# Attention's max pass as one stream of chunks, the output projection at a lower rate, background work held back while VectorE's modelled queue is long

## The chip, the core and the metric

The program runs on one core of one Trainium2 chip. The metric is the device time of one execution in microseconds, from the first to the last instruction of the core, launch included. Engines are called by the profile's names: PE (TensorE's matmuls; PEld are its weight loads), DVE (VectorE), ACT (ScalarE), POOL (GpSimd), SP (the queue that issues the DMAs). Each engine works off its own queue in order; between engines there are semaphores.

## What is computed

Two layers over 2048 latent tokens and 256 context tokens. A layer reads its stream through one input projection, and three groups of columns are mixed apart: a gated MLP over chunks (A), attention (B) and a linear recurrence in both directions (C). Their outputs, gated, go through `W_o`, and a layer norm closes the layer. The attention is this:

```python
def one_block(qblk):
    s = jnp.einsum('bqgrd,bkgd->bgrqk', qblk, k).astype(jnp.float32) * scale
    p = jax.nn.softmax(s, axis=-1).astype(v.dtype)
    return jnp.einsum('bgrqk,bkgd->bqgrd', p, v)
...
y = jnp.concatenate([mix_a * jax.nn.silu(a_g), attn * jax.nn.silu(b_g),
                     lru * jax.nn.silu(r_g)], -1) @ w_o
x_new = layer_norm(ALPHA * x + gate[:, None] * y, ln_g, ln_b)
```

There are 8 heads of 64 and 2 key heads; latent queries see 2304 keys, context queries 256. The context stream is only needed by the second layer, so the first layer has nine blocks of 256 queries and the second eight.

## The kernel before

A layer is a z phase (projection, gates, recurrence forward; `z_phase`) and an attention phase (`att_phase`), and only the second is touched. Values are kept as pairs of a high and a low half-precision part, which is why most products come as two or three matmuls.

**Units and steps.** A unit is one head of one block. A latent unit has nine steps, one for every two tiles of 128 keys; a context unit has one. So layer 0 has 584 steps and layer 1 has 576. A step `s` of the main loop writes, in this order:

- `scores` (L1023, L1024): four matmuls of 256 columns into a PSUM tile `stp`, then the exponential on ACT into `P`, which has six buffers (L1027);
- `low` (L1034): `Pl`, what `P` loses when its upper half is read as bfloat16. It runs on POOL or on DVE; `less_busy` chooses by the planner's clocks;
- `attend` of the step four earlier: eight matmuls into `pv` (L1051, L1053);
- pieces of other work, each a Python generator that is advanced so many times per step.

**The max pass.** The softmax needs each query's largest score before its exponential. `maxp(u)` is the generator of unit `u`: for each half of the 256 queries it multiplies against all keys in five chunks (four of 512 columns, one of 256) into PSUM tiles `sps`, of which there are three, and DVE reduces each chunk to `pm` (L940, L942) and the five to one column of `MZ` (L948). After the ten chunks come five empty advances, then two small matmuls `mp` and a copy (L954, L955) that put the negated maxima into row 64 of the query tile, where the score matmuls pick them up. `pace` advances the generators so that a unit's fifteen advances are done two steps before the unit begins; it looks four units ahead, and up to two advances fall into one step. `sps` also serves `mp` and the transposes `ytp`: PE waits when all three tiles are still to be read.

**The other work.** `wo` is the output projection of a block: per half block two tiles of 24 matmuls (L1144 to L1146), three per advance, then three DVE instructions per tile (L1149 to L1154); `affine` (L1161 to L1174) is the layer norm behind it. `wo_prep` makes the two halves of `W_o` (`OH` on ACT, `OL` on DVE, L884, 16 of these), and `wo` isn't advanced before `wo_prep` is done. `lru_back` is the backward recurrence: a scan and a cast on DVE (`hb` L859, `yc` L837) and two POOL instructions (L849, L850) per item. `ahead` (layer 0 alone) prepares the next layer: a first block's input, weights `wh_cc`/`wl_cc`, and `setup` with its small tables (`lwf` by DMA, then `lwh`, `lwl`; L235 to L244). `Rate` turns a number into advances per step: 0.8 for `wo`, 0.5 for `affine`, 0.13 for `lru_back`, 0.35 for `wo_prep`, 0.8 for `ahead`. Two switches empty a generator at once: `wo_prep` at step 136, `lru_back` at step 260.

**The planner's clocks.** `use(engine, cost)` adds an estimated time in us to `vt[engine]`; an engine never lies behind `vt[PE]`. In the kernel before only `less_busy` reads these clocks. They exist while the program is built; on the chip the order is fixed: within the attention phase the four engines get their instructions in the order in which they were written.

## Time and profile before

| | us |
|---|---|
| median of 3 runs | 2898.5 (2898.18 to 2899.23) |
| the profiled execution | 2900.0 |
| its span (first to last instruction) | 2897.9 |
| layer 0, first to last step (584) | 662.9 to 1498.4 |
| layer 1, first to last step (576) | 2076.0 to 2862.0 |
| PE busy | 2699.2 (93%) |
| DVE busy | 1995.7 (69%) |
| POOL busy | 1778.6 (61%) |
| ACT busy | 1342.6 (46%) |

Steps are found in the trace by their score matmuls: the first of every four `stp` matmuls marks a step's start. A stretch of the trace is then named by its steps; "steps 0 to 144" of layer 0 are 662.9 to 861.9 us, of layer 1 2076.0 to 2278.0 us. Matmuls overlap their neighbours, so a matmul's listed duration is longer than the time it takes from the engine; that time is read from one start to the next.

### The profile page before, as it was taken

The page shows a single profiled execution, that of the slowest core. Times are in us where ns is not written, and L with a number is a line of the kernel's source. Part 1 is how long each engine was busy: PE and PEld are TensorE (multiplying, and loading weights), DVE is VectorE, ACT ScalarE, POOL GpSimd, SP SyncE. Part 2 cuts the span into 40 slices and gives each one's busy share as a digit, 9 for nine tenths or more (in the row PEclk, how much of TensorE's full clock was granted, in tenths as well). Part 3 has the DMA queues.
Part 4 walks back from the last instruction along what each step waited for, and adds up shares of the span by engine and source line. Part 5 has one row for each costly group of instructions (what it writes and reads, how often), then busy time and mean ns, then how long its engine had stood idle before and what let it go on. Part 6 is the DMA issues. An engine that isn't in the chain of part 4 may idle for free. (4 is left out here: it accounts for less than half of the span.)

```text
span 2897.9 us, 60732 instructions
## 1 busy us (share of the span) xinstructions
PE 2699.2 (93%) x24121; PEld 1818.4 (63%) x24121; DVE 1995.7 (69%) x4000; ACT 1342.6 (46%) x2513; POOL 1778.6 (61%) x1825
## 2 busy tenths in 40 slices
PE   7999999898899999999998989998879999999998
PEld 3555555556677776777664655554567777777775
DVE  5565554558987777777877565555798876777775
ACT  3444433455544554445433454444555444544452
POOL 3244433347888786677764344334588877887774
PEclk9999999999999999999999999999999999999999
DMA  8232222115331110111114111110433110111001
GB/s 291 89 101 87 94 87 86 50 63 175 118 86 37 45 56 30 60 63 41 49 63 138 46 61 54 64 61 31 146 104 104 58 52 20 49 49 49 23 24 45
DMA packets 113717, 213.61 MB, mean 74 GB/s; under 512 B 13396, under 2 KB 45016, under 8 KB 113432
## 3 DMA queue, kind: packets, MB, share of 16 engines
q1 hardware_dynamic: 111060, 208.84, 21.7%
q8 instruction: 189, 3.10, 0.5%
q10 hardware_dynamic: 2372, 0.89, 0.1%
q14 instruction: 96, 0.79, 0.1%
HBM read 147.54 MB, written 62.14 MB: 72 GB/s over the span
## 5 line engine op out<-in xcount | busy, mean ns | idle before, releaser
L1034 POOL TENSOR_TENSOR Pl<-P 128x512 f16<-128x512 f32 x1131 | 1221.5, 1097 | 336.2 <-ACT P L1027 328.1
L1027 ACT ACTIVATE P<-stp 128x512 f32<-128x512 f32 x1160 | 692.5, 597 | 786.2 <-PE stp L1024 718.4
L942 DVE TENSOR_REDUCE pm<-sps 128x1 f32<-128x256 f32 (+1 forms) x1276 | 751.4, 627 | 272.3 <-PE sps L940 269.5
L1024 PE MATMUL stp<-aQB,KB 65*128 65x256 f16 x2320 | 582.7, 276 | 1.4 <-ACT aQB L955 1.4
L1023 PE MATMUL stp<-aQS,KK 128*128 128x256 f16 x2320 | 580.5, 275 | 0.0
L1051 PE MATMUL pv<-VX,P 128*128 128x129 f16 x4640 | 561.2, 220 | 0.0
L1053 PE MATMUL pv<-VX,Pl 128*128 128x65 f16 x4640 | 529.2, 193 | 6.6 <-DVE Pl L1034 3.5
L940 PE MATMUL sps<-KK,aQS 128*128 128x256 f16 (+1 forms) x1276 | 460.0, 362 | 58.9 <-DVE pm L942 56.2
L1053 PEld LDWEIGHTS <-Pl 128*128 128x128 f16 x4640 | 416.8, 98 | 100.4 <-DVE Pl L1034 4.8
L1051 PEld LDWEIGHTS <-P 128*128 128x128 bf16 x4640 | 431.4, 98 | 63.0 <-issue 48.4
L1024 PEld LDWEIGHTS <-KB 65*128 65x128 f16 x2320 | 228.9, 99 | 92.8 <-issue 2.5
L1023 PEld LDWEIGHTS <-KK 128*128 128x128 f16 x2320 | 230.9, 100 | 83.9 <-issue 14.0
L484 POOL TENSOR_SCALAR xh<-xm 128x512 f16<-128x512 f32 x68 | 45.0, 662 | 290.6 <-ACT xm L481 290.0
L495 PEld LDWEIGHTS <-xh 128*128 128x128 f16 x1040 | 102.4, 98 | 124.5 <-issue 19.0
L497 PEld LDWEIGHTS <-xl 128*128 128x128 f16 x1040 | 102.3, 98 | 122.7 <-issue 2.9
L496 PEld LDWEIGHTS <-xh 128*128 128x128 f16 x1040 | 102.3, 98 | 115.4 <-issue 9.2
L646 PE MATMUL cps<-xh,wh_cc 128*128 128x256 f16 x528 | 149.0, 282 | 3.3 <-POOL xh L484 3.0
L648 PE MATMUL cps<-xh,wl_cc 128*128 128x256 f16 x528 | 148.5, 281 | 3.3 <-DVE wl_cc L158 3.3
L647 PE MATMUL cps<-xl,wh_cc 128*128 128x256 f16 x528 | 148.8, 282 | 0.5 <-DVE xl L485 0.5
L397 POOL TENSOR_SCALAR gt<-gt,sp 128x256 f32<-128x256 f32 x72 | 43.9, 618 | 144.1 <-ACT gt L394 138.2
L940 PEld LDWEIGHTS <-aQS 128*128 128x128 f16 x1276 | 125.6, 99 | 10.3 <-DVE yB L1074 0.2
L719 ACT ACTIVATE uv<-uv 128x512 f32<-128x512 f32 x34 | 21.4, 630 | 207.7 <-DVE uv L718 207.7
(273 smaller groups left out, 5383.1 us busy)
## 6 DMA issues: line engine op xcount, KB each, us to landing
wf<-in_w_in_dram SPq DMA_DIRECT2D x64, 256.0 KB
wga<-in_w_ada_dram SPq DMA_DIRECT2D x32, 512.0 KB
lr<-LRd SPq DMA_DIRECT2D x32, 512.0 KB
SBd<-sbg SPq DMA_DIRECT2D x34, 256.0 KB
QSd<-QS SPq DMA_DIRECT2D x17, 512.0 KB
LRd<-gt SPq DMA_DIRECT2D x34, 256.0 KB
aQS<-QSd SPq DMA_DIRECT2D x17, 512.0 KB
asb<-SBd SPq DMA_DIRECT2D x17, 512.0 KB
```

The source lines that it names most:

```text
L495: T.matmul(ps[:, :w], xh[:, k, ts], wh[:, k, c0:], start=(k == 0), stop=False)
L646: T.matmul(ps, wh[:, k, cs], xh[:, k], start=(k == 0), stop=False)
L647: T.matmul(ps, wh[:, k, cs], xl[:, k], start=False, stop=False)
L648: T.matmul(ps, wl[:, k, cs], xh[:, k], start=False, stop=(k == KC - 1))
L940: T.matmul(ps[:, :w], QS[:, h, t * 128:(t + 1) * 128], KK[:, kv].rearrange("p a b -> p (a b)")[:, k0:k0 + w], start=True, stop=True)
L942: V.tensor_reduce(pm[:, i:i + 1], ps[:, :w], axis=AX, op=OP.max)
L1023: T.matmul(ps[:, i], KK[:, kv, kt], QS[:, h], start=True, stop=False)
L1024: T.matmul(ps[:, i], KB[:, kv, kt], QB[:, h], start=False, stop=True)
L1027: S.activation(P, ps, AF.Exp)
L1034: less_busy(0.6, 1.04, 2.0).tensor_tensor(Pl, P, Ph, op=OP.subtract)
L1051: T.matmul(pv[:, t, 0:129], Ph[:, i, ts], VX[:, kt, kv, 0:129], start=first, stop=False, skip_group_check=True)
L1053: T.matmul(pv[:, t, 64:129], Pl[:, i, ts], VX[:, kt, kv, 64:129], start=False, stop=end, skip_group_check=True)
```

## The change

The max pass is no longer one generator per unit. `stream` yields the chunks of all units one after the other, with no empty advances, and appends the unit to `rows`; `row_out`, called once per step behind the scores, counts three steps down and then writes the unit's `mp` matmuls and the copy (`max_row`). `pace` aims at five steps before the unit's beginning instead of two, looks three units ahead instead of four, and carries at most three advances over.

`Rate` now advances at most once per call and takes an argument `room`: where it is false nothing is advanced, and what is due is kept, up to three. `room(dv, po)` compares the planner's clocks: DVE's less than `dv` us ahead of PE's and POOL's less than `po`. The rates go to 0.64 for `wo` (0.8 before), 0.45 for `wo_prep`, 0.14 for `lru_back`; the order of the last three is changed, and the switch for `lru_back` stands at step 330.

The costs of `use` are new for most DVE work: a chunk of 512 0.60 us (0.59), `OL` 1.1 (0.6), scan and copy 1.2 (0.4), `yc` 0.65 (0.33), an affine instruction 1.05 (0.9), `wl_cc` 1.0 (0.6), a POOL pair of the recurrence 1.8 (1.4). `less_busy` gets (0.8, 1.06, 0.8) for (0.6, 1.04, 2.0): `Pl` goes to DVE when POOL is behind by 0.54 us more than DVE, not 1.56.

No instruction's shape changes, and PE, ACT and SP get the same number of each; DVE gets 42 of the 1160 `Pl`, 29 before.

```diff
-                for t in range(2 if u else 0):
+                for t in range(2):
                     pm = p.tile([128, 5], F32, name="pm", tag="pm", bufs=4)
...
-                        if i < 5 or t == 0:
-                            yield
-                    V.tensor_reduce(mz[:, t, 64:65], pm[:, :i], axis=AX, op=OP.max, negate=True)
-                    use(DV, 0.08)
-                for _ in range(5 if u else 0):
-                    yield
+                        if k0 + 512 >= nk:
+                            V.tensor_reduce(mz[:, t, 64:65], pm[:, :i], axis=AX, op=OP.max, negate=True)
+                            use(DV, 0.1)
+                        yield
...
-                less_busy(0.6, 1.04, 2.0).tensor_tensor(Pl, P, Ph, op=OP.subtract)
+                less_busy(0.8, 1.06, 0.8).tensor_tensor(Pl, P, Ph, op=OP.subtract)
...
+            def stream():
+                for u in range(1, len(units)):
+                    for _ in max_chunks(u):
+                        yield
+                    rows.append([u, 3])
...
+            def row_out(now):
+                for r in list(rows):
+                    r[1] -= 1
+                    if r[1] <= 0 or r[0] <= now:
+                        max_row(r[0])
+                        rows.remove(r)
+                        made[0] = r[0]
...
-                def __call__(self, gens):
-                    self.due += self.rate
-                    n = int(self.due)
-                    self.due -= n
-                    pump(gens, n)
+                def __call__(self, gens, room=True):
+                    self.due = min(self.due + self.rate, 3.0) if gens else 0.0
+                    if self.due >= 1.0 and room:
+                        self.due -= 1.0
+                        pump(gens, 1)
+
+            def room(dv, po=9.0):
+                return vt[DV] - vt[PE] < dv and vt[PO] - vt[PE] < po
...
-                total += 14 if b else 7
-                need[u] = total + 1
-            pumped, due = need[0], 0.0
+                total += (10 if b else 2) if u else 0
+                need[u] = total
+            pumped, due = 0, 0.0
...
-                for u in range(u0 + 1, min(u0 + 5, len(units))):
-                    rate = max(rate, (need[u] - pumped) / max(begin[u] - 2 - s, 1))
-                due += rate
+                for u in range(u0 + 1, min(u0 + 4, len(units))):
+                    rate = max(rate, (need[u] - pumped) / max(begin[u] - 5 - s, 1))
+                due = min(due + rate, 3.0)
...
                     if not preps:
-                        rwo(wos)
+                        rwo(wos, room(2.5))
                         if len(wos) > 1:
                             rwo(wos)
-                    rln(lnq)
-                    if len(lnq) > 1:
-                        rln(lnq)
-                    rback(backs)
-                    rprep(preps)
+                    rln(lnq, room(1.6) or len(lnq) > 1)
+                    rprep(preps, room(1.0))
+                    rback(backs, room(1.0, 2.0))
```

**DVE's queue in layer 0, around step 57.** `pm` are the chunk reductions, `OL` the weights' low half, `hb`, `hbk` and `yc` the recurrence, `rc`, `pv` and `yB` the end of a head. Before:

```order
L884 SCALAR_TENSOR_TENSOR OL<-wof,OH 128x512
L942 TENSOR_REDUCE pm<-sps 128x1 x2
L948 TENSOR_REDUCE MZ_77<-pm 128x1
L1070 RECIPROCAL rc<-pv 128x2
L1071 TENSOR_TENSOR pv<-ol,pv 128x2x64
L1074 SCALAR_TENSOR_TENSOR yB<-pv,rc,asb 128x64 x2
L884 SCALAR_TENSOR_TENSOR OL<-wof,OH 128x512
L837 SCALAR_TENSOR_TENSOR yc<-hb,yc 128x256
L859 SCALAR_TENSOR_TENSOR hb<-lr,hbk 128x256
L863 COPY hbk<-hb 128x1
L942 TENSOR_REDUCE pm<-sps 128x1
```

and now, around step 45, at the first scan of the recurrence in the same layer:

```order
L942 TENSOR_REDUCE pm<-sps 128x1 x3
L947 TENSOR_REDUCE MZ_75<-pm 128x1
L942 TENSOR_REDUCE pm<-sps 128x1 x2
L859 SCALAR_TENSOR_TENSOR hb<-lr,hbc 128x256
L863 COPY hbk<-hb 128x1
L942 TENSOR_REDUCE pm<-sps 128x1
L1036 TENSOR_TENSOR Pl<-P 128x512
L942 TENSOR_REDUCE pm<-sps 128x1 x2
L947 TENSOR_REDUCE MZ_75<-pm 128x1
```

Nine other instructions stood between two reductions; now the pieces of `wo_prep` and `lru_back` stand apart, with reductions between.

**POOL's queue at the start of layer 0's attention**, `Pl` and the pairs of the recurrence. Before:

```order
L1034 TENSOR_TENSOR Pl<-P 128x512 x23
L849 TENSOR_TENSOR hb<-lr 128x256
L850 TENSOR_TENSOR hb<-hb,lr 128x256
L1034 TENSOR_TENSOR Pl<-P 128x512 x6
L849 TENSOR_TENSOR hb<-lr 128x256
L850 TENSOR_TENSOR hb<-hb,lr 128x256
L1034 TENSOR_TENSOR Pl<-P 128x512 x6
```

and now:

```order
L1036 TENSOR_TENSOR Pl<-P 128x512 x21
L849 TENSOR_TENSOR hb<-lr 128x256
L850 TENSOR_TENSOR hb<-hb,lr 128x256
L1036 TENSOR_TENSOR Pl<-P 128x512 x21
L849 TENSOR_TENSOR hb<-lr 128x256
L850 TENSOR_TENSOR hb<-hb,lr 128x256
L1036 TENSOR_TENSOR Pl<-P 128x512 x26
```

The recurrence's pairs have moved from every sixth or seventh `Pl` to every twentieth or so, that is, to later steps.

**DVE's queue at the end of layer 0**, behind the last steps. `lwf` is the tile that is set to zero and filled by four DMAs, `lwh` and `lwl` are made of it, `yt` and `wops` belong to the last block's projection. Now:

```order
L1098 SCALAR_TENSOR_TENSOR yt<-ytp,yt 128x512 x2
L243 CAST lwh<-lwf 128x512
L244 TENSOR_TENSOR lwl<-lwf,lwh 128x512
L235 MEMSET lwf 128x512
L243 CAST lwh<-lwf 128x512
L244 TENSOR_TENSOR lwl<-lwf,lwh 128x512
L1157 BN_STATS st_20792<-r 128x6
L1151 TENSOR_TENSOR wops<-wops,gB 128x512
```

Before, ten chunk reductions and a projection's instructions stood between that MEMSET and the CAST behind it; the whole group has moved behind the last `yt`.

## Rows read from the trace of the kernel before

**Rows 1.** The page: busy us and share of the span, instructions, TensorE

```profile
PE 2699.2 (93%) x24121; PEld 1818.4 (63%) x24121; DVE 1995.7 (69%) x4000; ACT 1342.6 (46%) x2513; POOL 1778.6 (61%) x1825
```

**Rows 2.** By stretch: us, busy per engine (x instructions), clock, DMA share, GB/s

```profile
662.90:861.90 199.00, 178.58 (x1998) 136.57 (x1998) 176.22 (x344) 107.45 (x201) 173.16 (x165) 0.97 0.37 117
861.90:1008.30 146.40, 142.75 (x1592) 108.12 (x1591) 112.65 (x235) 74.03 (x139) 119.66 (x117) 1.00 0.16 50
1008.30:1498.40 490.10, 471.35 (x5021) 348.15 (x5020) 371.97 (x811) 234.77 (x454) 362.19 (x356) 0.99 0.15 47
2076.04:2278.00 201.96, 179.60 (x1997) 137.87 (x1996) 179.40 (x345) 107.48 (x201) 173.52 (x165) 0.96 0.32 104
2278.00:2423.00 145.00, 142.66 (x1593) 108.19 (x1592) 109.72 (x231) 73.42 (x137) 117.33 (x115) 1.00 0.15 48
2423.00:2862.00 439.00, 431.06 (x4768) 324.24 (x4767) 318.08 (x671) 215.43 (x402) 348.43 (x340) 1.00 0.11 37
```

**Rows 3.** PE's waits, layer 1, steps 0 to 144: us in total, times, longest

```profile
PE sps L940 <- DVE pm L942: 20.0, 16, 2.0
```

**Rows 4.** PE's waits, layer 1, steps 252 to 576: us in total, times, longest

```profile
PE sps L940 <- DVE pm L942: 6.0, 10, 1.5
```

**Rows 5.** Timeline, DVE and PE, layer 1: start, us, instruction, count, idle before

```profile
2149.82 2.21 DVE L942 TENSOR_REDUCE pm<-sps 128x1 f32<-128x512 f32 x4
...
2154.27 1.53 DVE L884 SCALAR_TENSOR_TENSOR OL<-wof,OH 128x512 f16<-128x512 f32 x1
...
2155.72 1.27 DVE L942 TENSOR_REDUCE pm<-sps 128x1 f32<-128x512 f32 x2
...
2156.45 0.38 PE L940 MATMUL sps<-KK,aQS 128*128 128x512 f16 x1 [0.39 <-DVE pm L942]
```

**Rows 6.** Timeline of PE alone, layer 1, a stretch without waits

```profile
2370.06 0.38 PE L1144 MATMUL wops<-OH,ayc 128*128 128x512 f16 x1
2370.28 0.38 PE L1145 MATMUL wops<-OL,ayc 128*128 128x512 f16 x1
...
2371.61 0.27 PE L1023 MATMUL stp<-aQS,KK 128*128 128x256 f16 x1
...
2372.40 0.27 PE L1023 MATMUL stp<-aQS,KK 128*128 128x256 f16 x1
...
2373.64 0.28 PE L954 MATMUL mp<-idH,MZ 128*65 128x128 f16 x2
2373.76 0.38 PE L940 MATMUL sps<-KK,aQS 128*128 128x512 f16 x1
2373.97 0.22 PE L1051 MATMUL pv<-VX,P 128*128 128x129 f16 x1
```

**Rows 7.** By stretch, as Rows 2: the first 36 steps of layer 0

```profile
662.90:703.70 40.80, 39.41 (x453) 30.92 (x453) 33.73 (x68) 25.75 (x47) 36.05 (x35) 0.92 0.48 170
```

**Rows 8.** DVE by form, layer 1, steps 0 to 144: busy, mean ns, idle

```profile
L942 DVE TENSOR_REDUCE pm<-sps 128x1 f32<-128x512 f32 x131 | 84.3, 683 | 15.6 <-PE sps L940 15.3
L884 DVE SCALAR_TENSOR_TENSOR OL<-wof,OH 128x512 f16<-128x512 f32 x16 | 17.8, 1112 | 0.0
L859 DVE TENSOR_TENSOR_SCAN hb<-lr,hbk 128x256 f32<-128x256 f32 x14 | 17.5, 1251 | 0.0
...
L837 DVE SCALAR_TENSOR_TENSOR yc<-hb,yc 128x256 f16<-128x256 f32 x14 | 10.6, 760 | 0.0
```

**Rows 9.** POOL's `Pl` and `hb`: layer 1, steps 36 to 108; 252 to 576; 0 to 144

```profile
L1034 POOL TENSOR_TENSOR Pl<-P 128x512 f16<-128x512 f32 x63 | 74.2, 1196 | 17.0 <-ACT P L1027 16.5 <-DVE pm L942 0.2
L849 POOL TENSOR_TENSOR hb<-lr,hb 128x256 f32<-128x256 f32 x10 | 8.3, 832 | 0.0
...
L1034 POOL TENSOR_TENSOR Pl<-P 128x512 f16<-128x512 f32 x322 | 342.6, 1081 | 89.8 <-ACT P L1027 88.2 <-ACT ol L1063 0.4
...
L1034 POOL TENSOR_TENSOR Pl<-P x130: 1033/1039/1562, 2078.2 to 2277.8; 128x512 f16<-128x512 f32 x130
```

**Rows 10.** Timeline of SP, end of layer 0: half of the second `lwf`'s issue

```profile
1460.52 1.25 SPq L238 DMA_DIRECT2D lwf<-in_lru_wr_dram  x2
```

More of the change, by code (lines that the diff above doesn't have):

```diff
@@ L837, in lru_back @@
                         V.scalar_tensor_tensor(yc[:, 1], hb, ysc(b) * HS, yc[:, 0], op0=OP.mult, op1=OP.subtract)
-                        use(DV, 0.33)
+                        use(DV, 0.65)
                         nc.sync.dma_start(YCd[b][:, :, cc], yc)
@@ L850, in lru_back @@
                         G.tensor_tensor(hb, hb, lr[:, 1], op=OP.mult)
-                        use(PO, 1.4)
+                        use(PO, 1.8)
                     if i + 2 < n:
@@ L864, in lru_back @@
                                 hbl[cc] = hc
-                            use(DV, 0.4)
+                            use(DV, 1.2)
                     yield
@@ L884, in wo_prep @@
                         V.scalar_tensor_tensor(OL[:, k, qs], wfs[k][:, qs], WS, OH[:, k, qs], op0=OP.mult, op1=OP.subtract)
-                        use(DV, 0.6)
+                        use(DV, 1.1)
                         yield
@@ L926, in load_ya, with max_chunks @@
                 yas[b] = (ya, yc)
-            def maxp(u):
+            def max_chunks(u):
                 b, h = units[u]
@@ L943, in maxp, with max_row @@
                         use(PE, w / 2370)
-                        use(DV, 0.06 + w / 960)
+                        use(DV, 0.2 + w / 1280)
                         i += 1
-                        if i < 5 or t == 0:
-                            yield
-                    V.tensor_reduce(mz[:, t, 64:65], pm[:, :i], axis=AX, op=OP.max, negate=True)
-                    use(DV, 0.08)
-                for _ in range(5 if u else 0):
-                    yield
+                        if k0 + 512 >= nk:
+                            V.tensor_reduce(mz[:, t, 64:65], pm[:, :i], axis=AX, op=OP.max, negate=True)
+                            use(DV, 0.1)
+                        yield
+            def max_row(u):
+                b, h = units[u]
+                mz = MZ[u % 3]
                 mp = pp.tile([65, TB], F32, name="mp", tag="sps", bufs=3)
@@ L982, in prep_ahead @@
                         V.tensor_tensor(xl[:, ks, ts], xm, xh[:, ks, ts], op=OP.subtract)
-                        use(DV, 0.6)
+                        use(DV, 0.95)
                         yield
@@ L1007, in load_w_ahead @@
                     V.scalar_tensor_tensor(wl[:, k], ws[k], WS, wh[:, k], op0=OP.mult, op1=OP.subtract)
-                    use(DV, 0.6)
+                    use(DV, 1.0)
             yBs, pvs, pls, exps = {}, {}, {}, []
@@ L1149, in wo @@
                         V.tensor_tensor(ps, ps, gB[:, ci, ns], op=OP.mult)
+                        use(DV, 0.65)
                         yield
                         V.scalar_tensor_tensor(r[:, ns], xt[:, ns], ALPHA, ps, op0=OP.mult, op1=OP.add)
-                        use(DV, 1.35)
+                        use(DV, 0.65)
                         yield
@@ L1171, in affine @@
                     V.scalar_tensor_tensor(r[:, qs], r[:, qs], mv[:, 0:1], lng[:, qs], op0=OP.subtract, op1=OP.mult)
-                    use(DV, 0.9)
+                    use(DV, 1.05)
                     yield
                     V.scalar_tensor_tensor(r[:, qs], r[:, qs], rv, lnb[:, qs], op0=OP.mult, op1=OP.add)
-                    use(DV, 0.9)
+                    use(DV, 1.05)
                     yield
@@ L1184, in att_phase @@
             steps = [(u, j) for u, (b, h) in enumerate(units) for j in range(NKT // 2 if b else 1)]
-            mx = [maxp(u) for u in range(len(units))]
-            def upto(u):
-                while len(units) - len(mx) <= u and mx:
-                    try:
-                        next(mx[0])
-                    except StopIteration:
-                        mx.pop(0)
+            rows, made = [], [0]
+            def stream():
[3 more added lines that the diff above has]
+                    rows.append([u, 3])
+            chunks = [stream()]
+            def row_out(now):
[5 more added lines that the diff above has]
+                        made[0] = r[0]
+            def upto(u):
+                while made[0] < u:
+                    if not any(r[0] == u for r in rows):
+                        pump(chunks, 1)
+                    else:
+                        row_out(u)
             class Rate:
@@ L1251, in att_phase @@
                 pump(backs, 1)
-                upto(0)
+                max_row(0)
                 for s in range(len(steps) + LAG):
+                    more = 0
                     if s < len(steps):
@@ L1260, in att_phase @@
                         scores(u, j)
+                        row_out(0)
                         more = pace(s)
                         if more:
-                            pump(mx, 1)
-                    else:
-                        more = 0
+                            pump(chunks, 1)
                     for g in list(outs):
@@ L1274, in att_phase @@
                     if more > 1:
-                        pump(mx, more - 1)
+                        pump(chunks, more - 1)
                     if not preps:
-                        rwo(wos)
+                        rwo(wos, room(2.5))
                         if len(wos) > 1:
                             rwo(wos)
-                    rln(lnq)
-                    if len(lnq) > 1:
-                        rln(lnq)
-                    rback(backs)
-                    rprep(preps)
+                    rln(lnq, room(1.6) or len(lnq) > 1)
+                    rprep(preps, room(1.0))
+                    rback(backs, room(1.0, 2.0))
                     if s == s0:
                         pump(preps, 1000)
-                    if s == 260:
+                    if s == 330:
                         pump(backs, 1000)
                     if s > s0:
-                        rlater(later)
+                        rlater(later, room(1.2, 2.5))
                 pump(outs, 100)
```

4 lines of the change are left out of this document (2 added, 2 removed).

## The prediction

> **What bounds the kernel now.** I read the page first, then the same table by stretch of steps, then PE's waits and the timeline. PE is busy for 93% of the span [rows 1], and only the attention phases are touched: 835.5 us in layer 0 and 786.0 us in layer 1 [rows 2]. The rows by stretch show two regimes. In steps 252 to 576 of layer 1, PE is busy for 431.1 of 439.0 us at a granted clock of 1.00: PE is the bound. In steps 0 to 144 of either layer PE is busy for 178.6 of 199.0 and 179.6 of 202.0 us, the clock is 0.97 and 0.96, and DVE is busy for 176.2 and 179.4 us, 89% of the time. There PE waits for DVE's chunk reductions, 20.0 us in 16 waits [rows 3], against 6.0 us in the three times as many steps of the quiet stretch [rows 4]. The timeline shows one such wait: four reductions end at 2152.0, then DVE works off other things until 2155.72, among them an `OL` of 1.53 us, and the next chunk's matmul on PE starts late [rows 5].
>
> **PE's floor.** To see what can be won I take PE's time without waits from start to start [rows 6]. A step without other work is 0.79 us (2371.61 to 2372.40); I use 0.795, since the two beside it differ by 0.01. A 512-column matmul is 0.215 (2373.76 to 2373.97; `wops` 2370.06 to 2370.28), a 256-column chunk half of that, 0.11; an `mp` 0.06; a transpose `ytp` I count like a 256-column matmul, 0.11. With the counts of the program's order before, the floor of a stretch is:
>
> - Steps 0 to 144: 144 x 0.795 + 130 x 0.215 + 33 x 0.11 + 96 `wops` x 0.215 + 32 x 0.06 + 8 x 0.11 = 169.5. Measured 199.0 and 202.0, so 29.5 and 32.5 are lost.
> - Steps 144 to 252: 108 steps, 96 + 24 chunks, 135 `wops`, 24 `mp`, 16 `ytp`: 141.4. Measured 146.4 and 145.0; lost 5.0 and 3.6.
> - Layer 0, steps 252 to 584: 332 steps, 278 + 85 chunks, 537 `wops`, 86 `mp`, 40 `ytp`, 16 transposes of the next layer's input: 459.9. Measured 490.1; lost 30.2.
> - Layer 1, steps 252 to 576: 324 steps, 278 + 69 chunks, 441 `wops`, 70 `mp`, 32 `ytp`: 427.5. Measured 439.0; lost 11.5.
>
> Together 112.3 us are lost, and that is all that an order can win. About 3.5 us of it per layer is the start, at a clock of 0.92 (40.8 us in layer 0 for a floor of 37.5 [rows 7]), which the change leaves alone.
>
> **Part 1, the chunks as a stream.** Before, the order of PE has two chunks in 126 of layer 0's first 288 steps and none in 89; now 252 of these steps have one, 36 two or three and none is empty. A reduction costs DVE 0.60 from start to start (two in 1.27 us [rows 5], less the 0.68 that one lasts [rows 8]), a step with one chunk costs PE 0.795 + 0.215 = 1.01. So DVE got 1.2 us of reductions in steps of 1.2 us and then none; now it gets 0.6 in each 1.01. There are three `sps` tiles, so DVE may be late by about three reductions, 1.8 us, before PE stops. `mp` now follows three steps behind its last chunk, which is enough for a reduction and `MZ`; I cost it at nothing. If that cover is gone, one `mp` is one wait of the size of a reduction, 0.6 us, per unit.
>
> **Part 2, background work held back.** The order now puts 4 items of the recurrence into layer 0's steps 0 to 144 instead of 15 scans and 14 casts, and no `wops` at all instead of 96, because `wo_prep` ends at its switch at step 136 (before around step 84). DVE's load there falls by 11 x 1.25 for scans and 11 x 0.76 for casts [rows 8], by about 10 for the projection's 3 tiles (9 instructions that stream like a reduction, 0.6, and 4 like `OL`, 1.1), and rises by 1.8 for three more chunks: 176.2 - 30 = 146 us. The floor of PE becomes 169.5 - 96 x 0.215 + 3 x 0.215 = 149.5. So DVE's share of the floor goes from 104% to 98%, and what is left of the excess is no longer in bursts. POOL's load is 131 `Pl` and 4 pairs: with 1.081 us and 2 x 0.83 per pair [rows 9] 148 us. All three engines are full at the same pace, so waits remain. Bounds for the loss: what the quiet stretch loses, 3% (4.5), and the start, is 8; 17%, as now with the start, is 25. I take 10, near the lower end, because the gate lets a background instruction out only while the planner sees less than 1.0 us queued on DVE, so with one instruction of 1.1 to 1.25 it is late by some 2.2 us against the 1.8 that the banks carry: 24 such instructions x 0.3 is 7, and the start. Gain: 199.0 - 20.0 (work moved out, net) - 159.5 = 19.5 in layer 0, 22.5 in layer 1.
>
> **Part 3, where the work goes.** Steps 144 to 252 get it: 192 and 198 `wops` instead of 135, floors 153.6 and 154.9; and 12 scans and 15 casts instead of 1 and 4, which with two more projection tiles, two affine instructions and five `Pl` brings DVE from 112.7 to about 144 us, 94% of the floor. I take a loss of 8 each, between 4 (now) and 26 (17%): -3.0 and -4.4.
>
> **Part 4, the rest of the layers.** In layer 1 after step 252 nothing moves but the chunks and the projection's rate; of 11.5 lost, 6.0 were waits for reductions [rows 4], and I leave 5: +6.5. In layer 0 the same, with the context units and the next layer's preparation, whose DVE work is now gated too: 30.2 becomes 15, between 10 and 25: +15.2.
>
> **Part 5, the ends.** Behind the last step stand 123 `wops` instead of 96 in layer 0, and 117 instead of 96 in layer 1. This is PE work that left the steps, 5.8 and 4.5 us, and is in the floors above; the last layer norm behind it is the same. In layer 0 DVE now has the second MEMSET of `lwf` right ahead of the CAST that needs its four DMAs. Their issue alone took 1.25 us for either two [rows 10], the landing isn't shown; before, ten reductions and a tile's projection work lay between. Behind that wait on DVE are the last blocks' `wops` multiplications, and SP's stores behind those, and the next layer's weight loads behind the stores. Up to four PSUM tiles of 24 matmuls (5.2 us each) keep PE going, so I take 2 of a possible 0 to 8: -2.
>
> Sum: 19.5 + 22.5 - 3.0 - 4.4 + 6.5 + 15.2 - 2 = 54.3. The profiled execution took 2900.0 us, so it becomes 2846; the median of the runs, 2898.5, stands 1.5 lower, so I forecast 2845 for the median.
>
> **The rivals.** (a) *The waits all but vanish.* If the banks and the gate cover everything, losses fall to 6 per first stretch, 4 per second, 10 and 4 later, and nothing at the end: 23.5 + 26.5 + 1 - 0.4 + 20.2 + 7.5 = 78, that is 2820. For it: the costs in `use` now agree with the rows (`OL` 1.1 against 1.11, scan 1.2 against 1.25 [rows 8]). Against it: three engines at 97% or more.
>
> (b) *POOL takes the bound.* `Pl` took 1.196 us on the mean in steps 36 to 108 of layer 1, where DVE was busiest, from 1.033 to 1.562 over steps 0 to 144 [rows 9]. At that pace POOL needs 131 x 1.196 + 6.6 = 163 in steps 0 to 144, over the floor of 149.5, and the loss is 17 instead of 10: 14 us less in all, 2858. Against it: fewer scans and casts run beside POOL there than now. The Trainium skill, "SBUF — State Buffer", section "Who interferes with whom", says that a DVE instruction with two SBUF inputs and a GpSimd instruction that reads SBUF share one read interface, and that the second blocks until the first ends. The trace agrees in that the median of `Pl`, 1.039, lies at its minimum and the longest is 0.52 above it; by that rule 36 such DVE instructions (16 `OL`, 13 `Pl`, 4 scans, 3 casts) at 0.52 would bring POOL to 131 x 1.04 + 19 + 6.6 = 162, and the time to about 2855.
>
> (c) *DVE's share decides, not the order: slower.* Now a stretch with DVE near full loses 17% of its floor, one at 77% loses 3% [rows 2]. If that depends on the share alone, steps 0 to 144 still lose 25, and steps 144 to 252, then at 94%, lose 26 instead of 4: +4, +7, -21, -22, and the rest +6.5 + 15.2 - 2 leaves -12, that is 2911. It decides from about 22 us of loss in each of the four stretches (they lose 70.6 now, and the rest wins 19.7). Against it: the waits come in bursts of reductions, and those are gone from the order.
>
> (d) *The change isn't felt*, because the waits only change their place: 2898. The order shows that the chunks and the gate do what they say, so this needs a balance by chance.
>
> **How the numbers follow.** The forecast (2830 to 2862, with a loss of 7 to 14 per first stretch) gets 0.57, (a) 0.16, (b) 0.12 beyond that, (c) 0.09, (d) 0.06. The range reaches from somewhat below (a), 2814, to the point where steps 0 to 144 lose 19, the next 12, the rest 8 and 23, and the end of layer 0 costs 5: 10.5 + 13.5 - 7 - 8.4 + 3.5 + 7.2 - 5 = 14, 2885. About 0.2% (6 us) is what a measurement of this kernel can tell from no change. Faster by more: 0.57 + 0.16 + 0.12 = 0.85; within: 0.06; slower: 0.09.
>
> **What would show it.** Right: in steps 0 to 144 some 160 us instead of 199 and 202, the wait of `sps` for `pm` falls from 20.0 to under 8 us per layer there and to 2 or 3 us in steps 252 to 576, and the clock stays at 1.00 behind the start; steps 144 to 252 take about 162. (b) would show as waits of ACT's exponential or of `pv` for POOL's `Pl`, with a mean over 1.15. (c) would show as waits for `pm` of over 10 us in steps 144 to 252. The end of layer 0 shows a gap on DVE before `lwh`; if it is over 8 us, part 5 is wrong. The forecast is wrong as a whole if PE's waits for DVE fall and the time doesn't: then the z phase of layer 1 starts later against the last step than the 27 moved `wops` account for.

## The result, and the profile after

The changed kernel took 2865.6 us (median of 4 runs, 2864.65 to 2867.75), the kernel before 2898.9 beside it: a ratio of 0.9886, 95% interval 0.9874 to 0.9898. It is 33 us faster; forecast were 54. The profiled execution took 2865.7 us, its span 2863.9.

The stretches of [rows 2] in the changed kernel, same columns and same steps (layer 0 first):

```profile
664.25:830.46 166.21, 155.67 (x1904) 127.19 (x1903) 152.86 (x301) 102.69 (x190) 152.86 (x141) 0.97 0.27 88
830.46:994.75 164.29, 157.37 (x1653) 114.90 (x1651) 143.43 (x280) 77.36 (x151) 131.06 (x135) 0.99 0.31 93
994.75:1483.36 488.61, 470.99 (x5032) 348.44 (x5030) 378.89 (x800) 236.03 (x455) 357.23 (x355) 1.00 0.15 47
2069.69:2231.30 161.61, 152.76 (x1904) 125.06 (x1903) 149.21 (x304) 102.58 (x190) 151.49 (x141) 1.00 0.26 84
2231.30:2388.96 157.66, 156.11 (x1658) 114.67 (x1656) 138.40 (x274) 77.05 (x149) 133.50 (x135) 1.00 0.27 87
2388.96:2825.86 436.90, 431.77 (x4776) 325.56 (x4775) 328.62 (x672) 215.75 (x402) 345.06 (x340) 1.00 0.12 38
```

With the prediction's floors (the last two with the new order's counts: 12 more `wops`, three fewer chunks) the losses are:

| steps | floor | measured | loss before | loss forecast | loss measured |
|---|---|---|---|---|---|
| layer 0, 0 to 144 | 149.5 | 166.2 | 29.5 | 10 | 16.7 |
| layer 0, 144 to 252 | 153.6 | 164.3 | 5.0 | 8 | 10.7 |
| layer 0, 252 to 584 | 461.8 | 488.6 | 30.2 | 15 | 26.8 |
| layer 1, 0 to 144 | 149.5 | 161.6 | 32.5 | 10 | 12.1 |
| layer 1, 144 to 252 | 154.9 | 157.7 | 3.6 | 8 | 2.8 |
| layer 1, 252 to 576 | 429.4 | 436.9 | 11.5 | 5 | 7.5 |

Layer 1 came out as forecast. Layer 0 missed its forecast by 21 us, 12 of them behind step 252.

PE's waits in layer 1, steps 0 to 144, against [rows 3] (us in total, times, longest):

```profile
PE sps L940 <- DVE pm L942: 7.8, 14, 1.5
```

and in its steps 252 to 576, against [rows 4]; the copy of the maxima on ACT, `aQB`, is a new releaser:

```profile
PE sps L940 <- ACT aQB L957: 3.0, 7, 0.5
PE sps L940 <- DVE pm L942: 1.7, 5, 0.6
```

In layer 0's steps 144 to 252 the projection itself waits for DVE, as it did not there before; `wops` has one PSUM bank:

```profile
PE wops L1146 <- DVE r L1154: 3.6, 3, 2.2
PE sps L940 <- DVE pm L942: 2.9, 4, 1.3
```

Where the 12 us behind step 252 went shows in steps 288 to 360 of layer 0, where the eight one-step context units stand among the latent ones. That section took 108.25 us before and 115.82 now. The rows of the two kernels:

```profile
1058.45:1166.70 108.25, 100.62 (x1088) 75.09 (x1084) 80.41 (x201) 51.98 (x105) 77.10 (x77) 0.98 0.16 51
```

```profile
1043.81:1159.63 115.82, 101.97 (x1086) 75.19 (x1084) 82.01 (x203) 52.76 (x105) 75.41 (x75) 0.99 0.14 47
```

DVE is busy for 71% of it, so it isn't DVE's load. Of PE's waits there, those for the copy of the maxima have grown (before, 1.6 us in 2 waits):

```profile
PE sps L940 <- ACT aQB L957: 3.2, 5, 1.0
...
PE stp L1026 <- ACT aQB L957: 1.5, 4, 0.4
```

PE's timeline there (start, us, idle before and its releaser) shows chunks and `mp` taking turns at waiting:

```profile
1111.42 0.27 PE L956 MATMUL mp<-idH,MZ 128*65 128x128 f16 x2 [0.37 <-DVE pm L942]
...
1112.18 0.38 PE L940 MATMUL sps<-KK,aQS 128*128 128x512 f16 x1 [0.49 <-ACT aQB L957]
...
1113.34 0.27 PE L940 MATMUL sps<-KK,aQS 128*128 128x256 f16 x1 [0.43 <-DVE pm L942]
...
1114.59 0.38 PE L940 MATMUL sps<-KK,aQS 128*128 128x512 f16 x1 [0.98 <-DVE pm L942]
...
1115.75 0.27 PE L956 MATMUL mp<-idH,MZ 128*65 128x128 f16 x2 [0.34 <-DVE pm L942]
...
1116.54 0.59 PE L940 MATMUL sps<-KK,aQS 128*128 128x512 f16 x1 [0.52 <-ACT aQB L957]
```

`pace` looks three units ahead, and with one-step units among them three units are few steps: it lets no chunk out for three or four steps and then two or three in each of five or six, with one or two `mp` among them. The kernel before does much the same there: up to three chunks in a step (not two, as I said of its `pace`), with empty steps between.

### The profile page after: what moved, and what is told of

Read it like the earlier page. It is cut to its first block, busy times and chain, and to the rows that moved or that the text cites. A ratio compares the mean times of both kernels' runs of the same rounds, so it can differ in the third digit from the quotient of the medians.

```text
span 2863.9 us, 60755 instructions
## 1 busy us (share of the span) xinstructions
PE 2688.2 (94%) x24121; PEld 1816.1 (63%) x24121; DVE 2031.8 (71%) x4013; ACT 1341.6 (47%) x2513; POOL 1757.0 (61%) x1812
## 5 line engine op out<-in xcount | busy, mean ns | idle before, releaser
L1036 POOL TENSOR_TENSOR Pl<-P 128x512 f16<-128x512 f32 x1118 | 1197.8, 1089 | 310.9 <-ACT P L1029 304.9
L942 DVE TENSOR_REDUCE pm<-sps 128x1 f32<-128x256 f32 (+1 forms) x1276 | 777.1, 628 | 249.8 <-PE sps L940 246.5
L1025 PEld LDWEIGHTS <-KK 128*128 128x128 f16 x2320 | 229.6, 99 | 85.8 <-issue 21.9
L940 PEld LDWEIGHTS <-aQS 128*128 128x128 f16 x1276 | 125.1, 98 | 16.8 <-issue 2.1
```

The lines of the kernel that those rows point to most:

```text
L940: T.matmul(ps[:, :w], QS[:, h, t * 128:(t + 1) * 128], KK[:, kv].rearrange("p a b -> p (a b)")[:, k0:k0 + w], start=True, stop=True)
L942: V.tensor_reduce(pm[:, i:i + 1], ps[:, :w], axis=AX, op=OP.max)
L1025: T.matmul(ps[:, i], KK[:, kv, kt], QS[:, h], start=True, stop=False)
L1036: less_busy(0.8, 1.06, 0.8).tensor_tensor(Pl, P, Ph, op=OP.subtract)
```

## The experiments

Diffs are against the changed kernel unless said otherwise; times are medians, ratios go to the kernel before on the same chip.

**Which half gained: the stream, the gate, or what is held back.** First, the max pass of the changed kernel with everything else as before (the costs of the other work and `less_busy` too, not shown):

```diff
-                        rwo(wos, room(2.5))
+                        rwo(wos)
...
-                    rprep(preps, room(1.0))
-                    rback(backs, room(1.0, 2.0))
+                    rback(backs)
+                    rprep(preps)
...
-            rwo, rln, rback, rprep, rlater = (Rate(x) for x in (0.64, 0.5, 0.14, 0.45, 0.8))
+            rwo, rln, rback, rprep, rlater = (Rate(x) for x in (0.8, 0.5, 0.13, 0.35, 0.8))
```

> The chunk stream alone: rates, switches, costs and less_busy as in the kernel before, no gate. By its order the chunks lie as in the changed kernel (124 of the first 144 steps have one), but 96 wops, 15 or 16 scans and 14 yc stay in steps 0 to 144. My theory (stream and gate each do a part): DVE still has 176 us of work for a floor of 170 there, so a loss of about 20 instead of 29.5 and 32.5, steps 144 to 252 stay at 145, layer 1's steps 252 to 576 win 4 as in the changed kernel, and the context section (layer 0, steps 288 to 360) loses 8 as it does there: 2898.5 - 22 - 4 + 4, about 2876. Rival (the gate does it all): 2892 to 2900. Rival (the stream does it all): 2862 to 2868.

2917.5 us, ratio 1.0070 (1.0057 to 1.0082): slower than before by 19. Its steps 0 to 144 (layer 0, then 1) stay where they were:

```profile
659.51:858.71 199.20, 181.20 (x2000) 137.16 (x1999) 178.88 (x347) 107.12 (x201) 174.60 (x166) 0.97 0.36 117
...
2089.96:2290.05 200.09, 180.97 (x2001) 136.94 (x2000) 181.32 (x348) 107.17 (x201) 175.10 (x166) 0.97 0.33 105
```

The waits for reductions there became more, and shorter on the mean: 15.1 us in 20 waits in layer 1 against 20.0 in 16 [rows 3], and waits at `mp` joined them. Layer 0's steps 252 to 584 took 505.2 us instead of 490.1, and 6.9 of the 15.1 lie in the context section (115.2).

Second, the gate, rates and costs alone, with the generator per unit of the kernel before:

```diff
-            chunks = [stream()]
+            mx = [maxp(u) for u in range(len(units))]
...
-                for u in range(u0 + 1, min(u0 + 4, len(units))):
-                    rate = max(rate, (need[u] - pumped) / max(begin[u] - 5 - s, 1))
+                for u in range(u0 + 1, min(u0 + 5, len(units))):
+                    rate = max(rate, (need[u] - pumped) / max(begin[u] - 2 - s, 1))
```

> The gate, new rates and new costs alone; the max pass is the generator per unit of the kernel before, with chunks in twos and empty steps. By its order no wops stand in steps 0 to 144 and 192 or 195 in steps 144 to 252, 5 or 6 scans in the first stretch. My theory: the bursts of two chunks stay, so the first stretches lose about 20 each, and steps 144 to 252, with DVE near full, lose some 15 each: 2898.5 - 22 + 20, about 2896, with waits of sps for pm of over 10 us in steps 144 to 252. Rival (the gate does it all): 2862 to 2872.

2849.3 us, ratio 0.9827 (0.9814 to 0.9841). I had this the wrong way round: the gate alone gains 49 us, more than the whole change, and stream and gate together are worth about their sum (+19 - 49 = -30; measured -33). Its steps 0 to 144 and 144 to 252, layer 0 and layer 1:

```profile
660.06:819.69 159.63, 152.82 (x1902) 125.46 (x1900) 149.03 (x300) 103.16 (x191) 149.84 (x138) 0.98 0.27 90
819.69:980.81 161.12, 156.57 (x1656) 114.41 (x1654) 140.46 (x282) 77.49 (x150) 133.63 (x135) 1.00 0.30 95
...
2052.04:2215.27 163.23, 154.25 (x1902) 126.59 (x1902) 151.16 (x302) 102.99 (x190) 152.42 (x140) 0.97 0.26 84
2215.27:2376.72 161.45, 155.45 (x1653) 113.92 (x1651) 138.93 (x274) 76.71 (x149) 129.04 (x131) 1.00 0.28 85
```

With floors of 149.0, 154.3, 149.0 and 153.6 from its order that is a loss of 10.6, 6.8, 14.2 and 7.9, close to what I had forecast for the kernel that has the stream as well. The bursts of two chunks are all there and do little harm. The context section has its bursts of three and its empty steps, as before, and took 109.9 us, less than in the changed kernel:

```profile
1028.94:1138.83 109.89, 100.71 (x1088) 74.66 (x1087) 80.39 (x200) 51.78 (x104) 77.15 (x77) 1.00 0.15 49
```

Third, that kernel with nothing held back:

```diff
             def room(dv, po=9.0):
-                return vt[DV] - vt[PE] < dv and vt[PO] - vt[PE] < po
+                return True
```

> The gate-alone kernel with room always true: new rates, costs, switches and at most one advance per call stay, nothing is held back. By its order 78 wops and 16 scans with 16 yc stand in steps 0 to 144 again. Theory A (holding work back by DVE's modelled queue is what won the 49 us): steps 0 to 144 go back to about 190 from 160 and 163, steps 144 to 252 to about 147, the time to 2880 to 2900. Theory B (the lower rates won it): the time stays within 10 of 2849.

2887.0 us, ratio 0.9955 (0.9942 to 0.9967); steps 0 to 144 took 197.5 us in both layers. So holding work back carries 35 to 38 of the 49 us; 2901.0 - 2887.0 = 14 at most is left to rates, costs and the cap of one advance. In these steps DVE was busy for 182 and 180 us, no less than before [rows 2]: without the gate its load was simply back, and PE waited for `Pl` on POOL as well (5.7 us in 8 waits in layer 1). So the gate's gain is in the first place work moved out of these steps. No run moves the same work by lower rates alone, so what the moment of its release is worth beside that isn't shown.

**Look-ahead and the place of `mp`.** The context section gave the first edit, and two steps for `mp` came with it:

```diff
-                for u in range(u0 + 1, min(u0 + 4, len(units))):
+                for u in range(u0 + 1, min(u0 + 8, len(units))):
...
-                    rows.append([u, 3])
+                    rows.append([u, 2])
```

> The changed kernel with pace looking seven units ahead instead of three, and mp two steps behind its last chunk instead of three. The order differs in layer 0's steps 280 to 364: instead of runs of 2, 2, 3, 2 chunks and then none, one or two chunks in nearly every step. My theory (the bursts that the short look-ahead makes among the one-step context units cost the 8 us that this section lost): the section falls from 115.8 to about 107 us, layer 0's steps 252 to 584 from 488.7 to about 480, the time from 2865.5 to about 2857. Rival (the section's waits come from the context units' pv and mp in the three sps banks, however the chunks lie): the section stays at 113 to 118, the time within 2 of 2865.5. In the rest nothing is expected, or up to 5 us more if two steps are too few for mp.

2841.9 us, ratio 0.9806 (0.9789 to 0.9822): 24 us under the changed kernel, three times what I expected. Layer 0's steps 252 to 583 fell to 474.2. Next, `mp` one step later than in the changed kernel, with its look-ahead (`rows.append([u, 4])`):

> The changed kernel with one number changed: mp four steps behind its unit's last chunk instead of three. In the changed kernel the step that has two chunks (one in nine) is nearly always the one that gets the mp as well, so three of its PSUM tiles are of the kind sps, of which there are three; now the mp stands one step behind. My theory (this coincidence makes most of the remaining waits of sps for pm: in layer 0's steps 0 to 252 eight of the thirteen over 0.5 us stand directly behind an mp or in that step): waits of sps for pm in steps 0 to 144 fall from 9.6 and 7.8 us to about 5, and the time by 4 to 8 us, to about 2859. Rival (DVE is late by its total there, the place of mp doesn't matter): within 2 of 2865.5.

2899.2 us, ratio 1.0003 (0.9994 to 1.0012). Wrong in sign: this one number gives the whole gain back. From layer 0's step 252 to the last step of layer 1 the rows that are new or larger are the scores that wait for the copy of the maxima, 12.6 us in 36 waits (2.5 in 7 in the changed kernel), and `mp` itself, 7.7 in 14 (0.9 in 3):

```profile
PE sps L940 <- DVE pm L942: 14.9, 32, 1.5
PE stp L1026 <- ACT aQB L957: 12.6, 36, 1.2
...
PE mp L956 <- DVE pm L942: 7.7, 14, 1.1
```

The two parts apart: the long look-ahead with three steps (`u0 + 8`, `[u, 3]`),

> The changed kernel with the longer look-ahead alone (seven units), mp three steps behind its last chunk as in the changed kernel; its order differs from the changed kernel in layer 0 from step 280 on and in which step gets the mp. It splits the 24 us that look-ahead and two steps won together. Theory A (the look-ahead mends the context section, 14.5 us of the 24 stood in layer 0's steps 252 to 584): section 288 to 360 at about 106, the time about 2850. Theory B (the nearer mp did it, as the farther one cost 33): the section stays at 113 to 116 and the time at 2860 to 2866.

2883.9 us, ratio 0.9942 (0.9930 to 0.9955). The context section was mended (104.9 us), yet the time is 18 us over the changed kernel and 42 over the run with two steps (16 and 39 by the ratios). And two steps with the short look-ahead (`u0 + 4`, `[u, 2]`):

> The changed kernel with mp two steps behind its unit's last chunk instead of three; the look-ahead stays at three units, so the bursts among the context units stay. By its order mp now stands in the step ahead of the one with two chunks (77 of 84 times), in the changed kernel in that step (76 of 83), with four steps one behind (76 of 83). Theory A (order: with mp ahead of the two chunks the chunk behind them needs mp's PSUM tile, which ACT has freed; with mp behind them it needs the first chunk's, whose reduction DVE does after the end of a head): as good as the changed kernel or somewhat better outside the context section, 2850 to 2864. Theory B (the fewer steps between chunk and mp the better, 17 us a step): 2845 to 2850. Both are off if two steps are too few: then waits of mp for pm of over 10 us and a time over 2870.

2849.3 us, ratio 0.9831 (0.9818 to 0.9845). The context section alone stayed at 114.5 us here, so it is the look-ahead that mends it. So neither of theories A and B of the run before was the whole: each step between the last chunk and `mp` costs 16 (2 to 3) or 34 us (3 to 4) at the short look-ahead, and 42 (2 to 3) at the long one.

The order tells these apart better than the number of steps. A latent unit's ten chunks fall into nine steps, so one step has two. Counted in the traces, `mp` stands ahead of that step in the run just shown, in it in the changed kernel and with two steps and the long look-ahead, and one step behind it with four steps and with three steps and the long look-ahead (82 or 83 of some 90 units in each). From ahead to the same step costs 16 us, from the same step to the one behind 34 and 42.

Between the two runs with the long look-ahead the traces show where it goes. Over the steps of both layers, chunks waited for reductions for 43.0 us instead of 25.6 and for the copy of the maxima for 9.9 instead of 0.5, and `mp` for reductions for 4.2 instead of 0: 31 of the 33 us by which these steps are longer. With four steps against three at the short look-ahead the listed waits tell only 17 of 33. One of the waits, in the run that took 2883.9; first PE without `stp` and `pv`:

```profile
2200.24 0.38 PE L940 MATMUL sps<-KK,aQS 128*128 128x512 f16 x1
...
2200.90 0.28 PE L956 MATMUL mp<-idH,MZ 128*65 128x128 f16 x2
...
2202.34 0.27 PE L940 MATMUL sps<-KK,aQS 128*128 128x256 f16 x1 [1.17 <-DVE pm L942]
```

and DVE at the same time:

```profile
2198.68 1.49 DVE L1036 TENSOR_TENSOR Pl<-P 128x512 f16<-128x512 f32 x1
2200.10 0.68 DVE L942 TENSOR_REDUCE pm<-sps 128x1 f32<-128x512 f32 x1
2200.70 0.15 DVE L1072 RECIPROCAL rc<-pv 128x2 f32<-128x2 f32 x1
2200.89 0.29 DVE L1073 TENSOR_TENSOR pv<-ol,pv 128x128 f32<-128x128 f32 x1
2201.22 0.48 DVE L1076 SCALAR_TENSOR_TENSOR yB<-pv,rc,asb 128x64 f32<-128x64 f32 x2
2201.61 1.61 DVE L942 TENSOR_REDUCE pm<-sps 128x1 f32<-128x512 f32 x3
```

Two chunks and `mp` hold the three `sps` tiles, DVE is at the end of a head and at no reduction for 0.9 us, and the chunk right behind `mp` stops PE. The beat returns once per unit, though not each time with a wait. Three tries at what makes the place good or bad:

```diff
-                        scores(u, j)
                         row_out(0)
+                        scores(u, j)
```

(on the kernel with long look-ahead and two steps)

> The kernel with seven units of look-ahead and mp after two steps (2842), but the mp matmuls and their copy stand ahead of the step's scores instead of behind them, so that on ACT the copy comes ahead of that step's exponential. What should change: mp's PSUM tile is free some 0.6 us earlier, and the copy delays the exponential by 0.36. Theory: that kernel has hardly a wait for the copy left (0.5 us in layer 0's steps 252 to 583), so 2838 to 2846. Rival (the copy ahead of the exponential delays the steps): 2848 to 2860.

2842.6 us, ratio 0.9810 (0.9796 to 0.9823): no change, as expected. Then `mp` at the end of the same step, behind both its chunks:

```diff
                         scores(u, j)
-                        row_out(0)
...
                         pump(chunks, more - 1)
+                    if s < len(steps):
+                        row_out(0)
```

(on the same kernel, with `[u, 3]`, since the count now runs once more in the step of the last chunk)

> The kernel with seven units of look-ahead that took 2842, its mp matmuls in the same step of the main loop, but written at the end of that step, behind its second chunk, instead of ahead of both chunks. Theory A (order: behind the two chunks the next chunk must wait for the first one's reduction, which stands behind the end of a head on DVE): as slow as with mp one step behind, 2870 to 2890, with waits of sps for pm in steps 0 to 144 of 13 us or more per layer. Theory B (what counts is the number of steps from the last chunk to mp): 2842 to 2852, with waits of 7 to 9 us there.

2851.1 us, ratio 0.9833 (0.9819 to 0.9847). Theory A falls: behind both chunks of its step `mp` costs 9 us, not the 42 of one step more. The waits change their place: over both layers' steps the chunks waited for reductions for 12.3 us instead of 25.6, and `mp` for 10.6 instead of 0. Where the 9 us lie isn't shown: the profiled executions of the two runs took the same time over the steps, 1557.9 and 1558.0 us. In this run the same place reads:

```profile
2176.88 0.38 PE L940 MATMUL sps<-KK,aQS 128*128 128x512 f16 x1
...
2177.47 0.27 PE L956 MATMUL mp<-idH,MZ 128*65 128x128 f16 x2 [0.21 <-DVE pm L942]
...
2178.19 0.27 PE L940 MATMUL sps<-KK,aQS 128*128 128x256 f16 x1
```

The next step's scores now stand between `mp` and the chunk, and the chunk doesn't wait. Last, chunks in twos only, so that DVE has holes again:

```diff
-                n = int(due)
+                n = 2 * int(due / 2)
```

(on the kernel with long look-ahead and two steps)

> The stream with seven units of look-ahead and mp after two steps, as in the run that took 2842, but pace lets chunks out in twos only: a step has two or none. By its order 60 of the 82 background instructions on DVE in steps 0 to 144 then stand between reductions two steps apart, where the changed kernel has 70 of 73 between reductions of neighbouring steps and the gate-alone kernel has half in holes of three or four steps. Theory A (an even stream leaves DVE no hole, so each background instruction makes a chunk late; that is why the stream lost 16 us against the gate alone): layer 0's steps 72 to 144 fall from 88 to about 81, as with the gate alone, all in all 8 to 14 us: 2828 to 2834. Theory B (the holes don't matter, the stream lost elsewhere): 2840 to 2850.

2851.5 us, ratio 0.9828 (0.9815 to 0.9842). Layer 0's steps 72 to 144 took 85.8 us (88.2 in the kernel that it is made from, 80.9 with the gate alone), and the whole is 10 us slower than that kernel. Empty steps one at a time don't give DVE what the gate alone has; its holes of three or four steps were not tried.

**What makes DVE's other work long.** `Pl` on POOL is replaced by zeros:

```diff
-                less_busy(0.8, 1.06, 0.8).tensor_tensor(Pl, P, Ph, op=OP.subtract)
+                e = less_busy(0.8, 1.06, 0.8)
+                if e is G:
+                    e.memset(Pl, 0.0)
+                else:
+                    e.tensor_tensor(Pl, P, Ph, op=OP.subtract)
```

> The changed kernel, but where Pl falls to POOL it is filled with zeros instead of the difference, so the low part of the softmax's numerator is left out for those steps and POOL reads nothing for them. In the changed kernel OL takes from 0.683 to 1.56 us on DVE, 1.23 on the mean in layer 0, and DVE's own Pl 1.21. Theory A (an instruction with two inputs in SBUF is slowed on DVE while POOL reads, and this is part of what makes reductions late): OL and DVE's Pl fall to 0.68 to 0.75, DVE's busy time in steps 0 to 144 by some 14 us, the waits of sps for pm there from 9.6 and 7.8 us to under 4, and with POOL's 150 us gone the time by 10 to 20, to 2845 to 2855. Theory B (they are long for another reason): OL stays above 1.0 on the mean, and the time moves by less than 5.

2836.4 us, ratio 0.9777 (0.9764 to 0.9791), with steps 0 to 144 in 155.4 and 156.4 us. DVE in layer 0's steps 0 to 144 (busy, mean ns), in the changed kernel and with zeros:

```profile
L884 DVE SCALAR_TENSOR_TENSOR OL<-wof,OH 128x512 f16<-128x512 f32 x16 | 19.5, 1230 | 0.0
L1036 DVE TENSOR_TENSOR Pl<-P 128x512 f16<-128x512 f32 x13 | 15.7, 1211 | 0.0
```

```profile
L884 DVE SCALAR_TENSOR_TENSOR OL<-wof,OH 128x512 f16<-128x512 f32 x16 | 10.8, 683 | 0.1
L1040 DVE TENSOR_TENSOR Pl<-P 128x512 f16<-128x512 f32 x13 | 8.9, 682 | 0.0
```

Theory A holds: the same instructions take 0.68 us when POOL reads nothing for `Pl`. PE's waits for reductions there fell from 9.6 to 0.8 us. The run also takes 77 us of work off POOL in each of these stretches, so not all of the 29 us are DVE's; PE waited there for POOL itself for 0.3 us at most in the changed kernel.

**A faster version.** Two steps everywhere, the long look-ahead only around the context units:

```diff
-                for u in range(u0 + 1, min(u0 + 4, len(units))):
+                for u in range(u0 + 1, min(u0 + (4 if last or not 252 <= s < 400 else 8), len(units))):
...
-                    rows.append([u, 3])
+                    rows.append([u, 2])
```

> The changed kernel with mp two steps behind its unit's last chunk everywhere, and seven units of look-ahead only in layer 0's steps 252 to 400, where the context units are; elsewhere three, so that mp stands in the step ahead of the one with two chunks. It puts together the context section of one run (layer 0's steps 252 to 583 in 474.2 us) and the other stretches of another (161.8, 161.5, 162.0, 157.4, 432.5). Theory (the two parts are independent): 2849.3 less 10 for the context section, 2836 to 2842, and the section from step 288 to 360 at about 106 us. Rival (what the context section wins is given back behind it, where the last layer's preparation waits): 2845 to 2850.

2836.2 us, ratio 0.9788 (0.9772 to 0.9805), faster than both kernels, and than the gate alone (0.9827, 0.9814 to 0.9841). Its context section, against 115.82:

```profile
1034.15:1139.90 105.75, 101.47 (x1101) 75.89 (x1100) 80.53 (x203) 51.77 (x105) 78.47 (x78) 1.00 0.16 51
```

## Why the prediction was right, and where its sum was off

The sign, the range and, nearly, the gain in the first stretches were right. That the total came so close is in part luck: the gate alone won 49 us, almost the 54 that were forecast for both halves, and the stream, which the forecast had among the gains, took 16 of them back. The main case, 2830 to 2862, was missed by 4 us; rival (b)'s 2858 lay nearer, but not for its reason. That steps 0 to 144 would take "some 160 us" was right for layer 1 (161.6) and 6 short for layer 0 (166.2). The wait of `sps` for `pm` fell to 7.8 us in layer 1 and 1.7 in its steps 252 to 576, under the 8 and the 2 to 3 that I had named; in layer 0's first stretch it stayed at 9.6 (16.8 before). The granted clock, forecast at 1.00 behind the start, was 0.99 or 1.00 from step 144 on, but 0.97 in layer 0's first stretch. One reading was wrong, and nothing hangs on it: steps 252 to 576 are 2.25 times as many as 0 to 144, not three times.

- **Part 1, the stream**, was given credit that it didn't earn. I read the bursts of reductions as the cause of PE's waits, because a burst stood ahead of the stall that I looked at, one of 0.39 us [rows 5]. The gate alone kept the bursts and lost 10.6 and 14.2 us in the first stretches. Spread out alone the chunks left the first stretch at 199 and 200 us. The two prices that I set to nothing were the wrong ones: `mp` "three steps behind its last chunk" was costed at nothing, and moving it by a step is worth 16 to 42 us, 0.12 to 0.3 us per unit; that `pace` looks three units ahead I told and did not cost. My own bound, 0.6 us per unit if the cover is gone, was of the right kind; it should have been in the sum. With `mp` at two steps, gate and stream together took 2849.3 us, as long as the gate alone: the 16 us that the stream cost beside the gate were the place of `mp`.
- **Part 2, the gate**, carried the gain: 49 us, and 35 to 38 of them by the run that holds nothing back. The stretches of the gate alone lost 10.6 and 14.2 us, forecast 10. One term was short: DVE's load in layer 0's steps 0 to 144 was 152.9 us, not 146. I subtracted the moved scans and casts and left the rest at its length of before, but the rest became longer: `OL` 1.23 us on the mean and `Pl` on DVE 1.21 in the changed kernel. Before, the same rows were

```profile
L884 DVE SCALAR_TENSOR_TENSOR OL<-wof,OH 128x512 f16<-128x512 f32 x16 | 17.1, 1071 | 0.0
L1034 DVE TENSOR_TENSOR Pl<-P 128x512 f16<-128x512 f32 x14 | 12.5, 892 | 0.0
```

and these two make up 5.6 of the 7 us. The run with zeros shows that such instructions last longer while POOL reads. Layer 0 lost 4.6 us more there than layer 1: 1.8 of it are in the waits above, and the granted clock was 0.97 in this stretch and 1.00 in layer 1's.
- **Part 3** was right in sum: 10.7 and 2.8 us lost for 8 and 8. What I didn't see was which wait would come: `wops` for DVE to empty its one bank.
- **Part 4** was right in layer 1 (7.5 lost for 5) and is the step that failed in layer 0: 26.8 lost for 15. "In layer 0 the same, with the context units" was the sentence; the context section went from 12 to 20 us of loss, the remaining steps from 18 to 7. The look-ahead of `pace` is the term that I left out: seven units for three, alone, took the section from 115.8 to 104.9, and with them the waits for the copy of the maxima there went. That the bursts as such cost it isn't shown: with a generator per unit they are no smaller, and the section took 108.2 and, with the gate, 109.9.
- **Part 5**: from layer 0's last step to layer 1's first 8.7 us more, 5.8 forecast for the moved `wops` and 2 for the wait. DVE did wait 4.2 us ahead of the `lwh` behind the second MEMSET, well under 8:

```profile
1493.73 0.48 DVE L235 MEMSET lwf<- 128x512 f32 x1
1498.37 0.43 DVE L243 CAST lwh<-lwf 128x512 f16<-128x512 f32 x1 [4.16 <-DMA lwf<-in_lru_wi_dram]
```

Behind the last step 2.1 us were added, for 4.5 of moved `wops`.

Of the rivals, (c) was refuted: steps 144 to 252 ran with DVE busy for 87 and 88% of the time and lost 10.7 and 2.8 us, not 26. (b) as I had put it, POOL as the bound, didn't come: `Pl` on POOL had a mean of 1.13 us and PE hardly waited for it. But its mechanism was there, on the other engine.

Open: why `mp` one step behind the step with two chunks costs 34 to 42 us, and at the end of that step, behind both chunks, 9. Whom the chunk behind `mp` waits for differs from run to run: in the run with `mp` at the step's end it waits on the semaphore of ACT's copy for 76 of 134 units, with three steps and the long look-ahead for 12. And the stream without the gate was run with `mp` at three steps alone, so what it is worth there with `mp` at a better place isn't shown.

## What to carry to other kernels

When an in-order engine feeds the bounding one, look for the stretch where its load exceeds the bounding engine's floor, and hold background work back there: here that won 49 us. Evening out the foreground work lost 19 by itself; with the gate it won 13 over the gate alone (11 by the ratios), but only once `mp` and the look-ahead had been set anew. Of a step that is moved, cost the small things that share its buffers (here two short matmuls and a one-row copy in one of three PSUM tiles): once per unit of a beat they came to as much as the change. And test a rule of planning at the places where its unit changes size, as `pace` did at the one-step units.

## What the runs showed of the hardware

A two-input instruction on DVE, both inputs in SBUF, took 0.68 us while POOL filled `Pl` with zeros, and 1.23 on the mean, 1.56 at most, while POOL computed it; the scans of 256 columns 0.74 against 1.26. Reductions from PSUM kept their 0.68 in both runs. The Trainium skill, "SBUF — State Buffer", section "Who interferes with whom", says just that such an instruction contends with a GpSimd instruction that reads SBUF and not with one that only writes. The runs agree, and show that here both paid: `Pl` on POOL kept a median of 1.04 us, with a mean of 1.13. By these means DVE's 16 `OL`, 13 `Pl` and 4 scans of layer 0's steps 0 to 144 took some 18 us more than with zeros, and POOL's 130 `Pl` an estimated 12 us over their median.
